# Two of the four weight sums of a seven-product block made by adding transfers instead of VectorE

## The chip, the cores and the metric

The kernel runs on one core of one Trainium2 chip. The metric is the device time of one execution in microseconds (us), given as the median of several runs. The profile is one further execution of the same program, with every instruction recorded.

## What is computed

Two layers of a hybrid language model on 256 tokens of width 1024, in fp32. Each layer is a feed-forward, a mixer (in the first layer a gated delta rule beside a state-space scan, in the second a sparse attention), and another feed-forward, each followed by a layer norm. So four of the six stages are this:

```python
def swiglu(x, w_in, w_out):
    gate, up = jnp.split(x @ w_in, 2, axis=-1)
    return (jax.nn.silu(gate) * up) @ w_out
# x: 256 x 1024, w_in: 1024 x 5632, w_out: 2816 x 1024
```

Weights come from HBM once per execution, 34.6 MB for one feed-forward.

## The kernel before

**Precision.** TensorE multiplies in a reduced fp32 form, so each operand is split into a high half (`whi`, a rounded copy, made on ScalarE or VectorE) and a low half (`wlo = raw - whi`, always VectorE), and each product is made of three matmuls: high by high, high by low, low by high. Every weight of 128 x 1024 thus costs one copy and one subtraction (`split`, line 657).

**A feed-forward** (`ffn`, line 986). The 2816 hidden columns are taken in units of 256. Most units ("R") load their gate and up columns, split them and multiply them with all tokens. Two places of each stage ("S" in `PATTERN`, line 49) take 512 columns at once with `block` (line 916): a scheme of Strassen's kind that makes the 2 x 2 blocks of (tokens) x (columns gate, up) with seven products instead of eight. `PATTERN` has one string for the first stage (one unit ahead of the pattern) and one for the other three. Eight blocks run in all.

**A block.** With b11, b12 the gate and up columns of the first 512 rows of the weights, and b21, b22 those of the second 512, the products take these weights, in this order: b11, T1, b21, T3, b22, T2, T4. The sums are made in place, one on the other, on tiles of raw weights:

```python
T1:  left  += right    # b11 + b12
T3:  right += b22      # b12 + b22
T2:  left  += b22      # T1 + b22
T4:  left  += b21      # T2 + b21
```

Each is done twice, for the two halves of k (`h` = 0, 1). A tile `r1` holds left (b11, columns 0 to 1023) and right (b12); `r2` holds b21 and b22. So a block holds four `raw` tiles of 1 MB, and there are just four buffers of that name (`RAW = 4`, line 27): further weights can only be loaded when T4 has been split. Left goes through the chain: b11 split, T1 added, T1 split, T2 added, T2 split, T4 added, T4 split. Right: T1 must have read it, then T3 is added and split. In before all four sums are `tensor_tensor` on VectorE (lines 935 to 942), of 128 x 1024 fp32. A product is twelve matmuls of 512 columns, six for each half of k. In the trace they read `whi,x` and `wlo,x` (b11, b21, T4) or `whi,sgh`, `wlo,sgh` and `whi,sgl` (T1, T3, b22, T2, with the token sums' halves `sgh` and `sgl`).

**What sets the order.** The kernel is first recorded as a list of operations (`Plan.add`), then `Plan.order` (line 328) plays it through with prices for each operation (`price`), waiting times between engines and a fixed number of buffers, and writes out one order for each engine; `emit` (line 559, the line of all instructions in the profile) issues them so. Within an engine everything runs strictly in that order, and an instruction that waits holds up all behind it. Copies recorded for ScalarE may be given to VectorE (`alts`) if VectorE is free first. A table (`ORDER`) corrects priorities by number of operation. Split weights live in tiles `m4`, at most 24 of them (12 pairs) for weights (`QUOTAS`, "W").

**Queues.** All loads are issued by SyncE. GpSimd has little to do: masks, a few powers for the layer norms (`lnve`), some attention work.

Of the kernel before, what the change touches and what calls it, by code (L numbers as in the profile page):

```python
# [9 lines left out]
F32 = mybir.dt.float32  # L10
# [3 lines left out]
OP = mybir.AluOpType  # L14
# [4 lines left out]
P = 128  # L19
T = 256  # L20
D = 1024
# [11 lines left out]
    "ps": (2, "PSUM"), "mp": (2, "PSUM"), "acc": (4, "PSUM"),  # L33
}

QUOTAS = {"M": None, "S": (8, 8), "Z": (4, 4), "L": (4, 4), "G": (4, 4), "P": (5, 5), "Q": (5, 5), "D": (4, 4), "W": (12, 24)}

KEPT = ("L", "G")

# [6 lines left out]

KEEP_WARM = 5500

PATTERN = {1: "RRRSRSRR", 2: "RSRRSRR"}


def H3(t, h):
# [120 lines left out]
class Plan:  # L173
# [76 lines left out]
    def price(self, op, eng, fn, args, kw):  # L250
        def n(a):
            return a.ids.size
        ps = lambda a: isinstance(a, V) and a.t.space == "PSUM"
        if eng == "tensor":
            out, l, r = args[:3]
            if fn == "transpose":
                return 111.0
            N, M = r.ids.size, l.ids.size
            if l.dtype == F32R:
                return N * 0.4427  # L260
            if M <= 32:
                return max(107.0, N * 0.455)
            if M <= 64:
                return 63.0 if N <= 64 else max(146.0, N * 0.896)
            return N * 1.7708 if N > M else 235.0 if N == M else 224.0
        if fn == "dma_start":
            return 60.0
        N = n(args[0]) if isinstance(args[0], V) else n(args[1])
        if isinstance(args[1] if len(args) > 1 else None, V):
            N = max(N, n(args[1]))  # L270
        ptr = sum(isinstance(kw.get(k), V) for k in ("scale", "bias"))
        if eng == "scalar":
            rows = args[0].p1 - args[0].p0

            more = (340 if rows <= 32 else 125 if rows <= 64 else 0) if fn == "activation" and N > 128 else 0
            return N / 1.2 + (51 if ps(args[1]) else 93) + 93 * ptr + (93 if "accum_out" in kw else 0) + more
        if eng == "vector":
            src = [a for a in args[1:] if isinstance(a, V)]
            if fn in ("tensor_copy", "tensor_scalar") and not any(ps(a) for a in src) and not ps(args[0]):
                c = N / (1.92 if N > 256 else 0.96) + 68  # L280
            elif fn == "reciprocal":
                c = N * 4 / 0.96 + 68
            elif fn == "memset":
                c = N / 0.96 + 20
            else:
                c = N / 0.96 + 67
            if fn == "tensor_tensor" and args[1].ids.ndim == 3 and N == 240:
                c += 165
            if fn == "scalar_tensor_tensor":
                c += 62 * isinstance(args[2], V)  # L290
            elif fn == "tensor_scalar":
                c += 62 * sum(isinstance(a, V) for a in args[2:4])
            return c
        if args[-1] is OP.pow:
            return 1300.0 + 130.0 * N
        return max(250.0, {"tensor_tensor": N * 2.1 + 150, "memset": N * .83 + 36,
                           "affine_select": N * .9 + 180}.get(fn, N * 1.7 + 480))
# [30 lines left out]
    def order(self, caps):  # L328
        ops = self.ops
        for op in ops:  # L330
            if op.fn == "dma_start":
                a = op.args[0] if isinstance(op.args[0], V) else op.args[1]
                op.nbytes = (a.p1 - a.p0) * a.ids.size * 4
                if isinstance(op.args[1], V) and op.args[1].t.space == "DRAM":
                    op.nbytes *= 2
            op.ndep = len(op.deps)
            op.ready = 0.0
# [18 lines left out]
        ready = {e: [] for e in engs}  # L356
        free = {e: 0.0 for e in engs}
        table = None
        dma_free = 0.0
        partial = heavy = False  # L360
        run = 0
        last = None
# [5 lines left out]
        left = len(ops)  # L368
# [62 lines left out]
        while left:  # L431
            best = None
            for e in engs:
# [7 lines left out]
                for op in lst:  # L441
                    r = op.ready
# [5 lines left out]
                    st = (r if r > f else f)  # L448
# [62 lines left out]
                port = st + c  # L511
            op.start = st
            if fn == "dma_start":
                dma_free = max(dma_free, st + 1300) + op.nbytes / 360.0
                op.end = dma_free + 600
                free[e] = st + c
            else:
                op.end = st + c
                free[e] = st + c
# [63 lines left out]
class K:  # L583
    NT = 2
    LAG = 5

    def __init__(self, plan, ins, caps):
        self.nc = self.plan = plan
# [327 lines left out]
    def block(self, st, w, c0, c1):  # L916

        nc, V = self.nc, self.nc.vector
        raw = []
        for h in range(2):  # L920
            tiles = [self.plan.tile("raw", [P, 2048], F32, "raw", stream="W") for r in range(2)]
            for r, t in enumerate(tiles):
                for e, c in enumerate((c0, c1)):
                    k = 4 * r + 2 * h
                    nc.sync.dma_start(t[:, e * 1024:(e + 1) * 1024].rearrange("p (k n) -> p k n", k=2),
                                      w[:, k:k + 2, c:c + 512])
            raw.append(tiles)
        A, B, C, D = (self.bank(tag) for tag in ("ps", "ps", "mp", "mp"))
        e1, e2 = self.m4(1024, "e1"), self.m4(1024, "e2")
        lh, rh = slice(0, 512), slice(512, 1024)  # L930

        def form(n, h):
            (r1, r2), u, v = raw[h], slice(0, 1024), slice(1024, 2048)
            left = r1[:, u]
            if n == "T1":
                V.tensor_tensor(left, left, r1[:, v], OP.add)
            elif n == "T3":
                V.tensor_tensor(r1[:, v], r1[:, v], r2[:, v], OP.add)
            elif n == "T2":
                V.tensor_tensor(left, left, r2[:, v], OP.add)  # L940
            elif n == "T4":
                V.tensor_tensor(left, left, r2[:, u], OP.add)
            src = {"b21": r2[:, u], "b22": r2[:, v], "T3": r1[:, v]}.get(n, left)
            hi, lo = self.m4(1024, "whi", "W", F32R), self.m4(1024, "wlo", "W", F32R)
            self.split(hi, lo, src)
            return hi, lo
# [39 lines left out]
    def ffn(self, l, j, x, then):  # L986
# [62 lines left out]
        def flush(keep):  # L1049
            while len(todo) > keep:  # L1050
                f, g, wo = todo.pop(0)
                out_mm(0, f, g, wo)
                if f >= NF - self.LAG:
                    late.append((f, g, wo))
                else:
                    out_mm(1, f, g, wo)
        st = None
        s = NT
        for n, kind in enumerate(PATTERN[NT]):
            if n == 3:  # L1060
                self.mark = len(self.plan.ops) - 1
            if kind == "S":
                if st is None:
                    st = self.sums_of_tokens(x)
                go = self.block(st, w_in, s * 256, DFF + s * 256)
                next(go)
                wo = self.unit_rows(w_out, 2 * s, 2, 0, D) + self.unit_rows(w_out, 2 * s + 2, 2, 0, D)
                flush(0)
                todo += [(2 * s + f, g, wo[f]) for f, g in enumerate(next(go))]
# [1 line left out]
                continue  # L1071
            wg = self.unit_cols(w_in, s * 256, 256)
            wu = self.unit_cols(w_in, DFF + s * 256, 256)
            if s == NT:
                for m in range(NT):
                    wo = self.unit_rows(w_out, 2 * m, 2, 0, D)
                    todo += [(2 * m + e, gts[2 * m + e], wo[e]) for e in range(2)]
            banks = self.proj_two(x, (wg[0], wu[0], wg[1], wu[1]), ("ps", "ps", "mp", "mp"))
            wo = self.unit_rows(w_out, 2 * s, 2, 0, D)
            for e in range(2):  # L1080
# [1192 lines left out]
```

## Time and profile before

| | |
|---|---|
| runs before | 1091.55, 1091.64, 1092.85 us; median 1091.64 |
| profiled execution | 1091.2 us |
| its span, first to last instruction | 1089.5 us |
| granted TensorE clock | 0.999 |
| instructions | 16005 |

How to read the profile: engines are PE (matmuls), PEld (weight loads, beside PE), DVE (VectorE), ACT (ScalarE), POOL (GpSimd), SP (SyncE; its q stands for its queue). `wlo<-raw,whi 128x1024 x390` names what an instruction writes and reads, the shape and the count; a group's row has busy us, mean ns of one, then the engine's idle time before them and who ended it. A timeline's row has start and length in us; a wait's row has us in total, times, longest. A DMA issue's row ends with the median time from issue to landing.

### The profile page before, as it was taken

What the parts mean: (1) busy time and instruction counts of PE and PEld (TensorE: products, weight loads), DVE (VectorE), ACT (ScalarE), POOL (GpSimd) and SP (SyncE); (2) the same over time, 40 slices, a digit from 0 to 9 for tenths busy, and PEclk for the clock granted to TensorE, in tenths of its full rate; (3) what the DMA queues carried; (4) which work ended last, traced back from release to release, by engine and by line L of the source; (5) the groups of instructions that cost most, each with busy time, mean ns of one, the idle gap of its engine ahead of it and who ended that gap; (6) DMA issues with size and microseconds to landing.
All of it is one profiled execution on the core that took longest, in us unless ns stands there. A gap on an engine that the chain in (4) does not pass through costs nothing.

```text
span 1089.5 us, 16005 instructions
## 1 busy us (share of the span) xinstructions
PE 1076.1 (99%) x6132; PEld 907.0 (83%) x6132; DVE 968.5 (89%) x1471; ACT 634.7 (58%) x1066; POOL 49.1 (5%) x78
## 2 busy tenths in 40 slices
PE   8999999999999999999999999999999999999997
PEld 6888888788999788888888888888887678888886
DVE  7999996888979899999995999897888999999965
ACT  5665673489788544555573655564375765655540
POOL 0000300001000110000000000010001000000000
PEclk9999999999999999999999999999999999999999
DMA  9919395633652383458394609378464145285541
GB/s 331 325 31 335 116 341 171 215 116 104 213 191 100 116 302 114 164 178 285 109 340 169 222 11 332 132 239 276 155 197 152 59 136 192 79 282 182 208 140 39
DMA packets 135799, 201.52 MB, mean 185 GB/s; under 512 B 10077, under 2 KB 95530, under 8 KB 135722
## 3 DMA queue, kind: packets, MB, share of 16 engines
q1 hardware_dynamic: 135722, 200.50, 54.2%
q8 instruction: 48, 0.79, 0.3%
q14 instruction: 29, 0.24, 0.1%
HBM read 197.18 MB, written 1.07 MB: 182 GB/s over the span
## 4 chain that ended last, share of the span: by engine, by line
PE 93%; DVE 3%; DMA 2%; ACT 1%; issue 1%; SPq 0%; DVEq 0%; ACTq 0%
PE ps L559 38%; PE acc L559 33%; PE mp L559 22%; DMA raw<-in_ffn_w_in_dram 1%; DVE arena L559 1%; DVE wlo L559 1%; DVE qs L559 0%; SPq L559 0%; DMA arena<-in_ssd_a_log_dram 0%; ACT whi L559 0%; DVE h L559 0%; DVE P L559 0%; DVE F L559 0%; ACT L559 0%; DVE g L559 0%
## 5 line engine op out<-in xcount | busy, mean ns | idle before, releaser
L559 DVE TENSOR_TENSOR wlo<-raw,whi 128x1024 fp32r<-128x1024 f32 (+1 forms) x396 | 469.0, 1213 | 10.2 <-ACT whi L559 7.7
L559 ACT ACTIVATE whi<-raw 128x1024 fp32r<-128x1024 f32 (+1 forms) x356 | 361.1, 1050 | 136.6 <-DMA raw<-in_ffn_w_in_dram 55.2
L559 PE MATMUL acc<-whi,g 128*128 128x512 f32 x704 | 223.3, 390 | 0.0
L559 PE MATMUL ps<-whi,x 128*128 128x512 f32 (+1 forms) x608 | 169.9, 386 | 1.3 <-DVE whi L559 1.3
L559 PE MATMUL ps<-x,whi 128*128 128x512 f32 (+1 forms) x720 | 159.2, 343 | 1.0 <-ACT cv L559 0.9
L559 PEld LDWEIGHTS acc<-whi,g 128*128 128x128 f32 x704 | 132.3, 188 | 26.7
L559 PE MATMUL acc<-wlo,g 128*128 128x512 f32 x352 | 137.4, 390 | 0.0
L559 PEld LDWEIGHTS ps<-x,whi 128*128 128x128 f32 x720 | 123.0, 189 | 17.2 <-ACT cv L559 2.4
L559 PEld LDWEIGHTS ps<-whi,x 128*128 128x128 f32 x608 | 109.7, 188 | 23.7 <-DVE whi L559 2.1
L559 PE MATMUL ps<-x,wlo 128*128 128x256 f32 x544 | 98.9, 284 | 0.0
L559 PE MATMUL ps<-wlo,x 128*128 128x512 f32 (+1 forms) x304 | 95.0, 385 | 0.5 <-DVE wlo L559 0.5
L559 PEld LDWEIGHTS ps<-x,wlo 128*128 128x128 f32 x544 | 81.1, 191 | 2.2 <-issue 0.2
L559 PE MATMUL mp<-x,whi 128*128 128x512 f32 x336 | 80.8, 390 | 0.2 <-DVE g L559 0.2
L559 ACT ACTIVATE sg<-ps 128x256 f32<-128x256 f32 x56 | 21.3, 380 | 95.6 <-PE ps L559 95.5
L559 PEld LDWEIGHTS acc<-wlo,g 128*128 128x128 f32 x352 | 66.2, 188 | 12.8
L559 PEld LDWEIGHTS mp<-x,whi 128*128 128x128 f32 x336 | 62.9, 188 | 13.6 <-DVE g L559 0.6
L559 DVE TENSOR_TENSOR sg<-ps,sg 128x256 f32<-128x256 f32 x56 | 23.4, 419 | 48.0 <-ACT sg L559 47.6
L559 PE MATMUL acc<-whi,x 128*128 128x512 f32 x192 | 65.3, 406 | 0.1
L559 PEld LDWEIGHTS ps<-wlo,x 128*128 128x128 f32 x304 | 55.5, 188 | 11.1 <-DVE wlo L559 1.0
L559 DVE TENSOR_TENSOR raw<-raw,raw 128x1024 f32<-128x1024 f32 x48 | 57.9, 1228 | 0.2
L559 PE MATMUL mp<-x,wlo 128*128 128x256 f32 x336 | 44.2, 283 | 0.0
L559 PEld LDWEIGHTS mp<-x,wlo 128*128 128x128 f32 x336 | 42.2, 192 | 0.2
(293 smaller groups left out, 1535.2 us busy)
## 6 DMA issues: line engine op xcount, KB each, us to landing
raw<-in_ffn_w_out_dram SPq DMA_DIRECT2D x44, 1024.0 KB, 5.0
raw<-in_ffn_w_in_dram SPq DMA_DIRECT2D x88, 512.0 KB, 5.3
raw<-in_ffn_w_in_dram SPq DMA_DIRECT2D x42, 1024.0 KB, 8.0
raw<-in_hyb_w_in_dram SPq DMA_DIRECT2D x20, 1024.0 KB, 6.0
raw<-in_hyb_w_out_dram SPq DMA_DIRECT2D x8, 1024.0 KB, 5.9
raw<-in_nsa_w_in_dram SPq DMA_DIRECT2D x5, 1024.0 KB, 5.9
raw<-in_nsa_w_out_dram SPq DMA_DIRECT2D x4, 1024.0 KB, 5.1
w<-in_nsa_cmp_w_dram SPq DMA_DIRECT2D x8, 512.0 KB, 9.0
```

The lines of the kernel that those rows point to most:

```text
L559: r = getattr(getattr(nc, eng), fn)(*[res(a) for a in args], **{k: res(a) for k, a in kw.items()})
```

## The change

T1 and T3 are no longer added by VectorE. GpSimd issues a transfer from one part of the raw tiles to another that adds to its destination (`accum_op=OP.add`), one for T1 and one for T3 in each half of k: 32 of 512 KB in the program. T2 and T4 stay on VectorE, and so do the splits of all. The tiles keep their layout (`HOME` says `raw` for both), `PATTERN` becomes a list by stage with the same strings, and the same steps are recorded in the same order. The planner's prices get a place for such a transfer.

```diff
-            return 60.0
+            return 1000.0 if eng == "gpsimd" else 60.0
...
-                dma_free = max(dma_free, st + 1300) + op.nbytes / 360.0
-                op.end = dma_free + 600
+                if e == "gpsimd":
+                    add_free = max(add_free, st + 1300) + op.nbytes / 360.0
+                    dma_free += op.nbytes / 360.0
+                    op.end = add_free + 600
+                else:
+                    dma_free = max(dma_free, st + 1300) + op.nbytes / 360.0
+                    op.end = dma_free + 600
...
+    HOME = ("raw", "raw")
+    RSTREAM = "R"
+    BY_DMA = ("T1", "T3")
...
-            (r1, r2), u, v = raw[h], slice(0, 1024), slice(1024, 2048)
-            left = r1[:, u]
-            if n == "T1":
-                V.tensor_tensor(left, left, r1[:, v], OP.add)
-            elif n == "T3":
-                V.tensor_tensor(r1[:, v], r1[:, v], r2[:, v], OP.add)
-            elif n == "T2":
-                V.tensor_tensor(left, left, r2[:, v], OP.add)
-            elif n == "T4":
-                V.tensor_tensor(left, left, r2[:, u], OP.add)
-            src = {"b21": r2[:, u], "b22": r2[:, v], "T3": r1[:, v]}.get(n, left)
+            left, right = part["b11", h], part["b12", h]
+            to, more = {"T1": (left, right), "T3": (right, part["b22", h]), "T2": (left, part["b22", h]),
+                        "T4": (left, part["b21", h])}.get(n, (None, None))
+            if to is not None:
+                if n in self.BY_DMA:
+                    nc.gpsimd.dma_start(to, more, accum_op=OP.add)
+                else:
+                    V.tensor_tensor(to, to, more, OP.add)
+            src = part.get((n, h), right if n == "T3" else left)
```

Since the planner's prices change, all engines' orders are made anew. TensorE's differs only in few rows at the ends of blocks, SyncE's in two loads. VectorE's has the 32 adds fewer, and 6 more copies of `whi`, one of `sgh`, 4 of `e` and 7 of `g` that ScalarE made before. Three places follow; numbers behind names tell tiles apart.

GpSimd, around the two blocks of the second feed-forward, before (`lnve` are the layer norms' powers, `arena_3706` the mixer's small values):

```order
L559 TENSOR_TENSOR arena_3706<-arena_3706,mhalf_110 128x1 x3
L559 TENSOR_TENSOR lnve_4250<-lnve_4250,mhalf_110 128x1
L559 TENSOR_TENSOR lnve_4364<-lnve_4364,mhalf_110 128x1
L559 TENSOR_TENSOR lnve_5841<-lnve_5841,mhalf_110 128x1
L559 TENSOR_TENSOR lnve_5939<-lnve_5939,mhalf_110 128x1
```

And after the change, the same place (`raw_4476` and `raw_4548` are left and right of the first block's two halves of k, `raw_4522` and `raw_4593` its b21 and b22; T1 has one tile on both sides):

```order
L564 TENSOR_TENSOR lnve_4364<-lnve_4364,mhalf_110 128x1
L564 DMA raw_4476<-raw_4476 128x1024
L564 DMA raw_4476<-raw_4522 128x1024
L564 DMA raw_4548<-raw_4548 128x1024
L564 DMA raw_4548<-raw_4593 128x1024
L564 DMA raw_5012<-raw_5012 128x1024
L564 DMA raw_5075<-raw_5075 128x1024
L564 DMA raw_5012<-raw_5037 128x1024
L564 DMA raw_5075<-raw_5117 128x1024
L564 TENSOR_TENSOR lnve_5841<-lnve_5841,mhalf_110 128x1
```

Eight transfers stand between two layer norms. In the first block T3 of the first half (which must wait for T1's landing there, as it overwrites what T1 reads) comes ahead of T1 of the second half; in the second block both T1 come first.

VectorE, first block of the second feed-forward, from the low half of b11 to that of T1, before (`whi_4644` is T1's high half, `xf` and `sgl` belong to the token sums):

```order
L559 TENSOR_TENSOR wlo_4562<-raw_4476,whi_4534 128x1024
L559 TENSOR_TENSOR g_4486<-mp_4558,g_4486 128x128 x2
L559 TENSOR_TENSOR xf_4440<-xf_4455,xf_4440 128x512
L559 TENSOR_TENSOR wlo_4580<-raw_4183,whi_4316 128x1024
L559 TENSOR_TENSOR xf_4455<-xf_4455,xf_4440 128x512
L559 TENSOR_TENSOR sgl_4598<-xf_4440,sgh_4582 128x1024
L559 TENSOR_TENSOR xf_4455<-xf_4455 128x512
L559 TENSOR_TENSOR wlo_4611<-raw_4548,whi_4589 128x1024
L559 TENSOR_TENSOR raw_4476<-raw_4476 128x1024
L559 TENSOR_TENSOR sg_4628<-ps_4540,sg_4628 128x256
L559 TENSOR_TENSOR sgl_4642<-xf_4455,sgh_4614 128x1024
L559 TENSOR_TENSOR sg_4628<-ps_4569,sg_4628 128x256
```

And after (`whi_4626` is T1's high half):

```order
L564 TENSOR_TENSOR wlo_4562<-raw_4476,whi_4534 128x1024
L564 TENSOR_TENSOR g_4486<-mp_4558,g_4486 128x128 x2
L564 TENSOR_TENSOR xf_4440<-xf_4455,xf_4440 128x512
L564 TENSOR_TENSOR wlo_4581<-raw_4183,whi_4316 128x1024
L564 TENSOR_TENSOR xf_4455<-xf_4455,xf_4440 128x512
L564 TENSOR_TENSOR sgl_4599<-xf_4440,sgh_4583 128x1024
L564 TENSOR_TENSOR xf_4455<-xf_4455 128x512
L564 TENSOR_TENSOR wlo_4612<-raw_4548,whi_4590 128x1024
L564 TENSOR_TENSOR sgl_4629<-xf_4455,sgh_4615 128x1024
L564 TENSOR_TENSOR wlo_4644<-raw_4476,whi_4626 128x1024
L564 TENSOR_TENSOR sg_4639<-ps_4540,sg_4639 128x256
L564 TENSOR_TENSOR sg_4639<-ps_4569,sg_4639 128x256
```

The add of T1 is gone, its low half has moved ahead of the `sg` sums that empty the banks of the unit before, and eight rows now stand between b11's low half and T1's. On ScalarE the copy `whi_4626` likewise stands ahead of the four copies that empty those banks. Further on in this block the cast of T1's other half stands eleven rows behind `wlo_4644`, and T3's other low half six rows behind that cast.

VectorE, second block of the same stage, before (left of the two halves is `raw_5027` and `raw_5108`):

```order
L559 TENSOR_TENSOR wlo_5126<-raw_5027,whi_5090 128x1024
L559 CAST whi_5136<-raw_5108 128x1024
L559 TENSOR_TENSOR raw_5027<-raw_5027 128x1024
L559 TENSOR_TENSOR wlo_5147<-raw_5108,whi_5136 128x1024
L559 TENSOR_TENSOR raw_5027<-raw_5027,raw_5063 128x1024
L559 TENSOR_TENSOR wlo_5164<-raw_5027,whi_5151 128x1024
L559 TENSOR_TENSOR raw_5108<-raw_5108 128x1024
```

And after (left is `raw_5012` and `raw_5075`):

```order
L564 TENSOR_TENSOR wlo_5115<-raw_5012,whi_5094 128x1024
L564 TENSOR_TENSOR wlo_5129<-raw_5075,whi_5121 128x1024
L564 CAST whi_5155<-raw_5012 128x1024
L564 TENSOR_TENSOR wlo_5162<-raw_5012,whi_5155 128x1024
L564 TENSOR_TENSOR raw_5012<-raw_5012,raw_5037 128x1024
L564 TENSOR_TENSOR wlo_5184<-raw_5075,whi_5176 128x1024
```

Between b11's low half and the cast of T1, which reads what the transfer has added, one row is left.

More of the change, by code (lines that the diff above doesn't have):

```diff
@@ L34 @@
 }
[L36 removed]
+QUOTAS = {"M": None, "S": (8, 8), "Z": (4, 4), "L": (4, 4), "G": (4, 4), "P": (5, 5), "Q": (5, 5), "D": (4, 4), "W": (12, 24), "R": (8, 8)}
 KEPT = ("L", "G")
@@ L47 @@
 KEEP_WARM = 5500
-PATTERN = {1: "RRRSRSRR", 2: "RSRRSRR"}
+PATTERN = ["RRRSRSRR", "RSRRSRR", "RSRRSRR", "RSRRSRR"]
 def H3(t, h):
@@ L333, in order @@
                 op.nbytes = (a.p1 - a.p0) * a.ids.size * 4
-                if isinstance(op.args[1], V) and op.args[1].t.space == "DRAM":
+                if isinstance(op.args[1], V) and (op.args[1].t.space == "DRAM" or op.eng == "gpsimd"):
                     op.nbytes *= 2
@@ L358, in order @@
         table = None
-        dma_free = 0.0
+        dma_free = add_free = 0.0
         partial = heavy = False
@@ L918, in block @@
         nc, V = self.nc, self.nc.vector
-        raw = []
+        part = {}
         for h in range(2):
-            tiles = [self.plan.tile("raw", [P, 2048], F32, "raw", stream="W") for r in range(2)]
-            for r, t in enumerate(tiles):
+            for r in range(2):
+                pair = None
+                if self.HOME[r] == "raw":
+                    pair = self.plan.tile("raw", [P, 2048], F32, "raw", stream="W")
                 for e, c in enumerate((c0, c1)):
                     k = 4 * r + 2 * h
-                    nc.sync.dma_start(t[:, e * 1024:(e + 1) * 1024].rearrange("p (k n) -> p k n", k=2),
-                                      w[:, k:k + 2, c:c + 512])
-            raw.append(tiles)
+                    t = pair[:, e * 1024:(e + 1) * 1024] if pair is not None else self.m4(1024, "raw", self.RSTREAM)
+                    nc.sync.dma_start(t.rearrange("p (k n) -> p k n", k=2), w[:, k:k + 2, c:c + 512])
+                    part["b%d%d" % (r + 1, e + 1), h] = t
         A, B, C, D = (self.bank(tag) for tag in ("ps", "ps", "mp", "mp"))
@@ L1056, in flush, with first @@
                     out_mm(1, f, g, wo)
+        def first():
+            for m in range(NT):
+                wo = self.unit_rows(w_out, 2 * m, 2, 0, D)
+                todo.extend((2 * m + e, gts[2 * m + e], wo[e]) for e in range(2))
         st = None
         s = NT
-        for n, kind in enumerate(PATTERN[NT]):
+        self.count = getattr(self, "count", -1) + 1
+        for n, kind in enumerate(PATTERN[self.count]):
             if n == 3:
@@ L1066, in ffn @@
                 next(go)
+                if n == 0:
+                    first()
                 wo = self.unit_rows(w_out, 2 * s, 2, 0, D) + self.unit_rows(w_out, 2 * s + 2, 2, 0, D)
@@ L1073, in ffn @@
             wu = self.unit_cols(w_in, DFF + s * 256, 256)
[L1074 to L1077, printed above, removed]
+            if n == 0:
+                first()
             banks = self.proj_two(x, (wg[0], wu[0], wg[1], wu[1]), ("ps", "ps", "mp", "mp"))
```

## Prediction

> **What bounds the kernel now.** I read the page first, for the engines' shares of the span.
>
> ```profile
> span 1089.5 us, 16005 instructions
> PE 1076.1 (99%) x6132; PEld 907.0 (83%) x6132; DVE 968.5 (89%) x1471; ACT 634.7 (58%) x1066; POOL 49.1 (5%) x78
> PE 93%; DVE 3%; DMA 2%; ACT 1%; issue 1%; SPq 0%; DVEq 0%; ACTq 0%
> ```
>
> TensorE is busy for 99% of the span. Since ends of matmuls are modelled, that alone proves little, so the next view is what TensorE waits for, whole.
>
> ```profile
> PE ps L559 <- DVE whi L559: 1.3, 1, 1.3
> PE acc L559 <- POOL ones L559: 1.1, 1, 1.1
> PE ps L559 <- ACT cv L559: 0.9, 1, 0.9
> PE ps L559 <- DVE wlo L559: 0.5, 1, 0.5
> PE mp L559 <- DVE P L559: 0.4, 1, 0.4
> PE mp L559 <- DVE e L559: 0.3, 1, 0.3
> PE ps L559 <- ACT P L559: 0.3, 1, 0.3
> PE mp L559 <- DVE arena L559: 0.3, 1, 0.3
> PE mp L559 <- DVE g L559: 0.2, 1, 0.2
> ```
>
> All waits add up to 5.3 us. Those on VectorE are 1.3 + 0.5 (both once, for the first weights of the program), 0.4 + 0.3 (attention), and 0.3 + 0.2 at the `e` and `g` tiles, which blocks and their neighbours make. Only the last 0.5 us lies where the change works. The chain of waits shows the pace inside a block; this row is one run of 36 matmuls of 512 columns, the products with a11, T1 and a12:
>
> ```profile
> 529.61 8.16 PE ps L559 x36
> ```
>
> 8.16 / 36 = 0.227 us from one matmul to the next, without a hole. So in feed-forward stages the end is set by TensorE's own matmuls, and the change adds or removes none.
>
> How near VectorE is to being late is read from one block, the first one of the second feed-forward. The table by stages of 10 us gives busy times in the order PE, PEld, DVE, ACT, POOL, then the granted clock, the DMA share and GB/s:
>
> ```profile
> 450.00:460.00 10.00, 10.00 (x60) 8.90 (x59) 9.76 (x16) 5.83 (x11) 0.00 (x0) 1.00 0.25 92
> 460.00:470.00 10.00, 10.00 (x46) 8.28 (x45) 10.00 (x10) 4.74 (x7) 0.00 (x0) 1.00 0.00 0
> ```
>
> VectorE works 9.76 and 10.00 of 10 us; the DMA engines fall to a share of 0.25 and then to nothing, since all four `raw` buffers are held by the block. What VectorE's pace costs is seen by pairing the end of a low half (`wlo`) with the matmul that reads it, in the timelines of VectorE and TensorE:
>
> ```profile
> 454.90 1.23 DVE L559 TENSOR_TENSOR wlo<-raw,whi 128x1024 fp32r<-128x1024 f32 x1
> 468.39 0.39 PE L559 MATMUL ps<-wlo,sgh 128*128 128x512 f32 x1
> 480.24 1.23 DVE L559 TENSOR_TENSOR wlo<-raw,whi 128x1024 fp32r<-128x1024 f32 x1
> 483.35 0.39 PE L559 MATMUL mp<-wlo,x 128*128 128x512 f32 x1
> 539.93 1.22 DVE L559 TENSOR_TENSOR wlo<-raw,whi 128x1024 fp32r<-128x1024 f32 x1
> 547.36 0.39 PE L559 MATMUL mp<-wlo,x 128*128 128x512 f32 x1
> 131.20 2.36 DVE L559 TENSOR_TENSOR wlo<-raw,whi 128x1024 fp32r<-128x1024 f32 x2 [1.22 <-ACT whi L559]
> 136.06 0.39 PE L559 MATMUL mp<-wlo,x 128*128 128x512 f32 x1
> ```
>
> The low half of T1 (first half of k) is done at 456.13 and read at 468.39: a lead of 12.3 us. The block's last low half, of T4, is done at 481.47 and read at 483.35: a lead of 1.9 us. So VectorE loses 10 us against TensorE over this block, and yet nobody waits. The last low half of the second block of that stage has 547.36 - 541.15 = 6.2 us, that of the second block of the first feed-forward 136.06 - 133.56 = 2.5. VectorE is the second bound, close behind, but behind.
>
> **The change part by part.** *Adds removed.* The groups of instructions hold them:
>
> ```profile
> L559 DVE TENSOR_TENSOR raw<-raw,raw 128x1024 f32<-128x1024 f32 x48 | 57.9, 1228 | 0.2
> L559 DVE TENSOR_TENSOR raw<-raw 128x1024 f32<-128x1024 f32 x16 | 19.3, 1218 | 0.1
> L559 DVE CAST whi<-raw 128x1024 fp32r<-128x1024 f32 x39 | 26.6, 687 | 1.8 <-DMA raw<-in_ffn_w_in_dram 0.8 <-DMA raw<-in_ffn_w_out_dram 0.5
> L559 ACT ACTIVATE whi<-raw 128x1024 fp32r<-128x1024 f32 x351 | 357.1, 1053 | 136.1 <-DMA raw<-in_ffn_w_in_dram 55.2 <-DVE raw L559 35.1 <-DMA raw<-in_ffn_w_out_dram 33.9
> L559 DVE COPY PT<-mp 128x512 f32<-128x512 f32 x10 | 6.8, 686 | 2.2 <-PE mp L559 2.0
> L559 DVE CAST g<-sg 128x256 fp32r<-128x256 f32 x9 | 2.6, 291 | 0.2
> ```
>
> The 16 adds with one name on the right are T1 (both operands in one tile). The 48 are T2, T3 and T4, of which T3 is 16. So 16 x 1.218 + 16 x 1.228 = 39.1 us leave VectorE, 4.9 us a block. (Adds in a row start 1.13 us apart, so 4 x 1.13 = 4.5 us of a block's time.)
>
> *Copies moved.* With VectorE freer, the planner gives it more of the copies that ScalarE did: 6 of `whi` and one of `sgh` at 0.687 us (the cast's row), 4 of `e` and 3 of `g` with 512 columns at 0.686 (nearest row, the copy PT<-mp), 4 small ones of `g` at 0.291. That is 4.8 + 4.8 + 1.2 = 10.8 us back on VectorE. Net 39.1 - 10.8 = 28.3 us less: 968.5 becomes about 940.
>
> *Worth of that.* TensorE waits for VectorE 0.5 us in these stages, so the most that 28.3 us can buy is 0.5 us. The rest only lengthens leads. I take 0.3.
>
> *The transfers added.* 32 transfers of 512 KB from SBUF to SBUF that read the destination as well. No row of before is one, nor any transfer from GpSimd's queue. The nearest rows, with the time from issue to landing at the end:
>
> ```profile
> Y<-zeros SPq DMA_DIRECT2D x2, 512.0 KB, 3.8
> raw<-in_ffn_w_in_dram SPq DMA_DIRECT2D x88, 512.0 KB, 5.3
> raw<-in_ffn_w_in_dram SPq DMA_DIRECT2D x42, 1024.0 KB, 8.0
> w<-in_nsa_cmp_w_dram SPq DMA_DIRECT2D x8, 512.0 KB, 9.0
> ```
>
> Y<-zeros is a plain SBUF to SBUF transfer of that size: 3.8 us, the lower end (it can't be cheaper with a second read). Twice the bytes is like the 1024 KB rows, 8.0 us, and a crowded 512 KB takes 9.0, the upper end. During a block the DMA engines are mostly idle (0.25 and 0.00 above), so I start from the first row and add what 512 KB more cost from HBM: 3.8 + (8.0 - 5.3) = 6.5 us. L = 6.5 is an estimate, and GpSimd's issue is in it only so far as SP's is.
>
> [...]
>
> *What covers L.* In the first block of the second feed-forward the new order puts eight rows of VectorE between the low half of b11 and that of T1. They are in the trace of before, with their starts:
>
> ```profile
> 445.95 0.48 DVE L559 TENSOR_TENSOR g<-mp,g 128x128 fp32r<-128x128 f32 x2
> 451.56 1.21 DVE L559 TENSOR_TENSOR raw<-raw 128x1024 f32<-128x1024 f32 x1
> 453.33 1.22 DVE L559 TENSOR_TENSOR sgl<-xf,sgh 128x1024 fp32r<-128x1024 f32 x1
> 454.46 0.42 DVE L559 TENSOR_TENSOR sg<-ps,sg 128x256 f32<-128x256 f32 x1
> ```
>
> From 445.95 (the two `g`) to 451.56 is 5.61, and the last of them, `sgl`, takes 454.46 - 453.33 = 1.13: 6.7 us. ScalarE's high half of T1 (1.05 us) must fit in too, and hand-overs, so about 5.4 us of L are covered. The second place is T3 of the other half of k, with five rows between it and T1's cast there, so about 5.0 covered. The third is T1 of the other half, which GpSimd issues only after T3 of the first, so after the first landing: some 7 us. With L = 6.5 VectorE waits 1.1 + 1.5 + 0 = 2.6 us in such a block. Against that stand the 4.5 us of adds that are gone and a lead of 1.9, 6.4 us in all. The lead grows by some 2 us.
>
> In the second blocks only the low half of b11's other half (1.13 us) stands between. There VectorE stands still for L - 1.1 = 5.4 us, 0.9 more than the adds took (4.5), and the lead of 6.2 shrinks to 5.3.
>
> *Who is queued behind these waits.* On ScalarE, behind the high half of T1, stand the copies that empty four banks of the projection before. In before VectorE empties one of them at 452.99, and TensorE writes a `ps` bank again at 465.44:
>
> ```profile
> 452.99 0.42 DVE L559 TENSOR_TENSOR sg<-ps,sg 128x256 f32<-128x256 f32 x1 [0.22 <-ACT sg L559]
> 465.44 0.39 PE L559 MATMUL ps<-whi,x 128*128 128x512 f32 x1
> ```
>
> 12 us of room hide a wait of one. On GpSimd, behind a transfer that waits, stand only the block's other transfers; the powers of the layer norms come after a block's last one. On SP nothing moves but two weight loads by a few places. The next loads wait for the `raw` buffers, and these come free when T4's low half is done, as before or earlier.
>
> *Sum.* The profiled execution took 1091.2 us, 1.7 over its span, and the median of the three runs is 1091.64. 1091.64 - 0.3 + 0 = 1091.3 us. A measurement of this kernel tells about 0.2% (2.2 us) from no change, so this is no change.
>
> **The rivals.** *Slow landing: slower.* If L is larger, VectorE, in order, stands still with all other low halves behind the wait, and beyond the lead TensorE stops. In the first block of the second feed-forward it waits (L - 5.4) + (L - 5.0) + (L - 7.0), which reaches 6.4 at L = 7.9: from there on the time grows. At L = 9.0 (the crowded row) that block loses 3.2 us and the second block of the first feed-forward, whose lead is nearly as small (2.5), about 3: 1091.3 + 6 = 1097. At L = 10 these two lose 6 each and two further blocks 3 each: 1109. For it: no row shows an adding transfer, and the three waits add up. Against it: the DMA engines are mostly idle then, and the rows that read most like it stay under 7.9 save in a crowd. Chance 0.26.
>
> [...]
>
> *TensorE isn't the bound: faster.* The chain gives VectorE 3% of the span, of which the low halves of weights are:
>
> ```profile
> by line: PE ps L559 38.4%; PE acc L559 32.9%; PE mp L559 22.0%; DMA raw<-in_ffn_w_in_dram 1.3%; DVE arena L559 0.6%; DVE wlo L559 0.6%; issue 0.5%; DVE qs L559 0.5%; SPq L559 0.4%; DMA arena<-in_ssd_a_log_dram 0.3%; ACT whi L559 0.3%; DVE h
> ```
>
> 0.6% or 6.5 us. If these are real, relief of VectorE returns up to 6.5 us: 1085. [...] Against it stand the 0.227 us without a hole and the waits of 5.3 us; the chain steps aside into VectorE where TensorE goes on. Chance 0.07.
>
> *The order shifts something elsewhere.* A few TensorE rows swap places at each block's end, which is worth tenths. It stays in the forecast's case.
>
> **The numbers.** Forecast (no change) 0.67, slow landing 0.26, faster 0.07. Of the slow case about half lies above L = 9.3 (1099), 0.12 left out; below 1089.5 about 0.07. So the range is 1089.5 to 1099, and most of it is the slow case's; the forecast's own range is 1089.5 to 1093. Faster 0.07, same 0.67, slower 0.26.
>
> **What would show it.** In the profile of the changed kernel: `raw<-raw` with 16 gone from VectorE and 32 of `raw<-raw,raw` left, 45 casts of `whi`, VectorE near 940 us; 32 issues of 512 KB on POOL, landing after some 6.5 us; gaps of VectorE of some 5 us that end on those landings in the second block of the last three feed-forwards, and of 1 to 2 us in first blocks; TensorE's waits still near 5 us with `e` and `g` perhaps gone. I am wrong if TensorE waits for `whi` or `wlo` inside blocks (slow landing: look at the landing time, 8 us or more), or if the span drops by over 2.2 us (then TensorE's rows hid stalls).

## The result, and the profile after

| | before | after |
|---|---|---|
| median | 1092.24 us (4 runs, 1091.55 to 1094.99) | 1102.2 us (4 runs, 1099.69 to 1103.28) |
| profiled execution | 1091.2 us, span 1089.5 | 1102.02 us, span 1100.3 |
| granted TensorE clock | 0.999 | 0.996 |

The ratio is 1.0083 with a 95% interval of 1.0058 to 1.0108. The kernel is slower by 9 us, 0.8%, four times what a measurement can tell from no change. (Ratios and medians leave disturbed runs out, in all one of g2's; a ratio is not taken from the medians and can differ a little from theirs.)

The page of the changed kernel, for shares of the span, then its groups and its issue row for what was moved:

```profile
PE 1080.5 (98%) x6132; PEld 909.1 (83%) x6132; DVE 945.0 (86%) x1457; ACT 622.3 (57%) x1048; POOL 73.5 (7%) x110
```

```profile
L564 DVE TENSOR_TENSOR raw<-raw,raw 128x1024 f32<-128x1024 f32 x32 | 39.4, 1235 | 0.5
L564 DVE CAST whi<-raw 128x1024 fp32r<-128x1024 f32 x45 | 30.9, 689 | 28.3 <-DMA raw<-raw 19.2 <-DMA raw<-in_ffn_w_out_dram 6.9 <-DMA raw<-in_ffn_w_in_dram 1.8
```

```profile
raw<-raw POOLq DMA_DIRECT2D x32, 512.0 KB, 5.5
```

The edit did what it says: 32 adds are left, six more casts of `whi`, VectorE is busy for 945.0 us instead of 968.5, and 32 transfers land after 5.5 us in the median. But TensorE's waits, whole, are 11.6 us where they were 5.3, and the new ones have one name:

```profile
PE mp L564 <- DVE e L564: 4.6, 3, 2.6
PE ps L564 <- DVE e L564: 1.8, 1, 1.8
```

Where they lie is told by the table by stages (busy time of PE, PEld, DVE, ACT, POOL, then the granted clock, the DMA share and GB/s). Nearly all of the loss is in one place, the second block of the first feed-forward and the units behind it. Before:

```profile
120.00:130.00 10.00, 10.00 (x46) 8.29 (x45) 9.45 (x11) 6.26 (x8) 9.64 (x7) 1.00 0.41 85
130.00:140.00 10.00, 10.00 (x46) 8.29 (x45) 8.76 (x10) 3.30 (x4) 0.64 (x4) 1.00 1.02 354
140.00:150.00 10.00, 9.49 (x46) 7.27 (x44) 9.29 (x13) 8.75 (x11) 0.00 (x0) 1.00 0.94 317
150.00:160.00 10.00, 10.00 (x59) 8.94 (x60) 10.00 (x14) 7.79 (x14) 0.00 (x0) 1.00 0.97 350
```

After:

```profile
120.00:130.00 10.00, 8.21 (x33) 6.34 (x32) 9.97 (x10) 5.33 (x6) 6.79 (x10) 0.89 0.11 21
130.00:140.00 10.00, 10.00 (x43) 8.18 (x42) 9.02 (x11) 5.29 (x6) 0.00 (x0) 0.94 0.54 133
140.00:150.00 10.00, 8.47 (x40) 6.80 (x39) 6.11 (x9) 3.16 (x4) 0.00 (x0) 1.00 1.05 368
150.00:160.00 10.00, 7.39 (x28) 5.67 (x27) 9.96 (x12) 9.24 (x10) 0.00 (x0) 0.83 1.01 342
```

The slices count 144 matmuls in these 40 us instead of 197 (one that spans two slices counts in both). Two things besides its waits are to be seen. The granted clock is 0.89, 0.94 and 0.83 in slices that hold or follow a wait: it is 0.50, half of what it was, from 127.84 to 131.25 us and from 155.15 to 158.56. And the DMA engines, at a share of 1.02 from 130 to 140 before, are at 0.54: loads that should run there do not.

One number for each kernel helps below. I take the starts of TensorE's matmuls, and sum by how much each stands further from the next than is usual for its shape (the lower quartile, from 40 ns over it on); from 120 to 205 us this **stall** is 1.6 us before and 10.2 after. Over the whole program it is 58.0 and 68.8, so this place holds 8.6 of 10.8 us, and the span grew by 10.8. (Most of the rest, 1.3 us, is lost ahead of 40 us. The three waits shown below add up to 5.9 us; two times 3.41 us at half the clock lose another 3.4.)

What happens there, in order. GpSimd's issues (start, length, what it waited for), then ScalarE's first copy behind them:

```profile
104.75 0.86 POOL L564 DMA_DIRECT2D raw<-raw  x1 [41.71 <-DMA raw<-in_ffn_w_in_dram]
108.25 0.86 POOL L564 DMA_DIRECT2D raw<-raw  x1 [2.64 <-DVE sg L564]
114.25 0.86 POOL L564 DMA_DIRECT2D raw<-raw  x1 [5.14 <-DMA raw<-raw]
116.71 0.86 POOL L564 DMA_DIRECT2D raw<-raw  x1 [1.60 <-DMA raw<-raw]
```

```profile
113.98 1.06 ACT L564 ACTIVATE whi<-raw 128x1024 fp32r<-128x1024 f32 x1 [4.01 <-DMA raw<-raw]
```

T1's transfer of 104.75 lands only at 113.96, after 9.21 us (three loads of this block, which land at 107.64, 110.17 and 112.79, are under way too, and from 108.25 on T1's other transfer); that of T3 at 114.25 has no load beside it and lands after 4.65. ScalarE and VectorE stand still for about 4 us, so the sums on VectorE come later. T4's two adds, before:

```profile
125.61 2.35 DVE L559 TENSOR_TENSOR raw<-raw,raw 128x1024 f32<-128x1024 f32 x2
```

And after:

```profile
129.06 1.23 DVE L564 TENSOR_TENSOR raw<-raw,raw 128x1024 f32<-128x1024 f32 x1
132.67 1.22 DVE L564 TENSOR_TENSOR raw<-raw,raw 128x1024 f32<-128x1024 f32 x1
```

Before, the second starts at 126.75, right behind the first. The first is 3.5 us late, of which the kernel brought 1.3 along from its start; the second is 5.9 late, since the new order also puts two low halves between them. Then SyncE, before:

```profile
119.70 0.59 SPq L559 DMA_DIRECT2D arena<-in_gdn_conv_w_dram  x1
...
125.22 1.01 SPq L559 DMA_DIRECT2D arena<-in_hyb_w_in_dram  x2
126.90 1.50 SPq L559 DMA_DIRECT2D raw<-in_ffn_w_out_dram  x2
```

And after:

```profile
130.35 0.37 SPq L564 DMA_DIRECT2D raw<-in_ffn_w_out_dram  x1
130.84 0.59 SPq L564 DMA_DIRECT2D arena<-in_gdn_conv_w_dram  x1
...
136.55 1.06 SPq L564 DMA_DIRECT2D arena<-in_hyb_w_in_dram  x2
137.71 1.01 SPq L564 DMA_DIRECT2D raw<-in_ffn_w_out_dram  x1
138.83 1.03 SPq L564 DMA_DIRECT2D raw<-in_ffn_w_in_dram  x2
```

Before, eleven small loads for the next stage (`arena`) went out one after the other from 119.70 to 126.2, SyncE issued nothing else in between, and both w_out loads followed at 126.90 and 128.03, when T4's adds had freed their buffers. After, the first w_out load stands ahead of the eleven. It waits on SyncE until its buffer is free at 130.35, the eleven come behind it, and the second w_out load goes out at 137.71, 9.7 us later than before, though VectorE has read its buffer for the last time at 132.75. The three loads behind it follow in one heap. VectorE and TensorE, at the end of that block:

```profile
143.89 0.69 DVE L564 CAST whi<-raw 128x1024 fp32r<-128x1024 f32 x1 [4.67 <-DMA raw<-in_ffn_w_out_dram]
144.50 0.68 DVE L564 TENSOR_TENSOR e<-mp,e 128x512 f32<-128x512 f32 x1
147.37 0.68 DVE L564 TENSOR_TENSOR e<-ps,e 128x512 f32<-128x512 f32 x1
```

```profile
126.81 0.50 PE L564 MATMUL ps<-whi,x 128*128 128x512 f32 x1 [1.79 <-DVE e L564]
149.31 0.66 PE L564 MATMUL mp<-ident,e 128*128 128x128 f32 x4 [1.53 <-DVE e L564]
154.65 0.68 PE L564 MATMUL mp<-ident,e 128*128 128x128 f32 x4 [2.61 <-DVE e L564]
```

VectorE, in order, stands 4.67 us in front of a cast that needs the late load, the sums of `e` are behind it, and TensorE waits for these: 1.53 and 2.61 us. The wait of 1.79 us at 126.81 is another: the copy that empties the bank of a11 and a12 was ScalarE's before and now stands on VectorE behind two low halves.

### The profile page after: what moved, and what is told of

It is laid out like the page before. It is cut to its first block, busy times and chain, and to the rows that moved or that the text cites. A ratio compares the mean times of both kernels' runs of the same rounds, so it can differ in the third digit from the quotient of the medians.

```text
span 1100.3 us, 16129 instructions
## 1 busy us (share of the span) xinstructions
PE 1080.5 (98%) x6132; PEld 909.1 (83%) x6132; DVE 945.0 (86%) x1457; ACT 622.3 (57%) x1048; POOL 73.5 (7%) x110
## 3 DMA queue, kind: packets, MB, share of 16 engines
q0 software_dynamic: 4608, 16.78, 8.1%
## 4 chain that ended last, share of the span: by engine, by line
PE 88%; DVE 5%; DMA 3%; issue 1%; ACT 1%; SPq 0%; DVEq 0%; ACTq 0%
PE ps L564 37%; PE acc L564 31%; PE mp L564 21%; DVE wlo L564 2%; DMA raw<-in_ffn_w_in_dram 2%; DMA raw<-raw 1%; DMA raw<-in_ffn_w_out_dram 1%; DVE arena L564 1%; ACT whi L564 0%; DVE qs L564 0%; DVE e L564 0%; SPq L564 0%; DVE raw L564 0%; DVE h L564 0%; DVE whi L564 0%
## 5 line engine op out<-in xcount | busy, mean ns | idle before, releaser
L564 ACT ACTIVATE whi<-raw 128x1024 fp32r<-128x1024 f32 (+1 forms) x350 | 353.6, 1049 | 166.1 <-DMA raw<-raw 54.0
L564 DVE CAST whi<-raw 128x1024 fp32r<-128x1024 f32 (+1 forms) x46 | 31.5, 687 | 28.3 <-DMA raw<-raw 19.2
L564 POOL DMA_DIRECT2D raw<-raw x32 | 28.1, 891 | 360.7 <-DMA raw<-in_ffn_w_in_dram 210.4
```

Source lines behind the costliest of these rows:

```text
L564: r = getattr(getattr(nc, eng), fn)(*[res(a) for a in args], **{k: res(a) for k, a in kw.items()})
```

## The experiments

All ran beside the kernel before on the same chip; ratios are to it, with 95% intervals (in the four groups e, f, g and h it took 1092.55, 1094.01, 1092.14 and 1091.86 us). "SyncE's row" says whether the first w_out load stands ahead of the eleven small loads or behind them.

| run | transfers | SyncE's row | stall 120-205 | span over before | DMA share 130-140 | median us | ratio |
|---|---|---|---|---|---|---|---|
| before | 0 | behind | 1.6 | | 1.02 | 1092.24 | |
| after | 32 | ahead | 10.2 | 10.8 | 0.54 | 1102.2 | 1.0083 (1.0058 to 1.0108) |
| e1_not_first | 24 | behind | 1.0 | -0.2 | 1.02 | 1092.74 | 0.9997 (0.9982 to 1.0013) |
| e2_first_only | 8 | ahead | 7.1 | 10.2 | 0.71 | 1101.53 | 1.0078 (1.0054 to 1.0101) |
| e3_order_alone | 0 | ahead | 9.6 | 18.8 | 0.39 | 1111.16 | 1.0181 (1.0147 to 1.0214) |
| e4_transfers_alone | 64 | behind | 6.9 | 53.8 | 0.96 | 1147.89 | 1.0502 (1.0472 to 1.0533) |
| f4_transfers_32 | 32 | behind | 3.0 | 16.0 | 0.91 | 1109.38 | 1.0139 (1.0103 to 1.0175) |
| f1_copy_first | 32 | ahead | 7.1 | 5.8 | 0.76 | 1101.37 | 1.0070 (1.0048 to 1.0092) |
| f2_casts_behind | 32 | ahead | 7.4 | 10.1 | 0.63 | 1099.97 | 1.0050 (1.0034 to 1.0067) |
| f3_both | 32 | ahead | 9.4 | 10.0 | 0.57 | 1099.95 | 1.0051 (1.0031 to 1.0071) |
| g1_load_behind | 32 | behind | 3.0 | 2.9 | 1.02 | 1094.37 | 1.0035 (1.0016 to 1.0053) |
| g2_load_and_rows | 32 | behind | 3.2 | 4.4 | 0.94 | 1096.38 | 1.0042 (1.0019 to 1.0065) |
| g3_price_3000 | 32 | behind | 4.8 | 5.0 | 0.35 | 1099.29 | 1.0065 (1.0040 to 1.0091) |
| h1_before_load_ahead | 0 | ahead | 5.9 | 8.0 | 0.75 | 1098.74 | 1.0055 (1.0034 to 1.0077) |

The profiled span is set against before's 1089.5 us. f1's profile is of its fastest execution (1097.04 us) and g3's of one of its faster ones (1096.25), so their rows are low for their medians. The stall of this place is not all that the spans lose. Matched one by one with before, the 6132 starts of TensorE's matmuls in e2, f2 and h1 fall back by 2.9, 3.5 and 3.1 us more between 300 and 320 us, in the first layer's mixer: TensorE stands still there once, for 1.3 to 1.8 us, where the profile names no engine that it waits for, and the granted clock is 0.83 from 310 to 320 us (before 1.00). The changed kernel has none of it, and whether it belongs to these changes no run settles.

**Where.** Two kernels split the change by stage.

```diff
-                if n in self.BY_DMA:
+                if n in self.BY_DMA and self.count > 0:     # e1; in e2: == 0
```

> The two blocks of the first feed-forward keep all adds on VectorE; the six blocks of the other three make T1 and T3 by transfer. Theory A (the loss is local: in the first feed-forward's second block the transfers share the DMA engines with the block's own loads, land after 8 to 9 us, and the delay is handed on through the raw buffers to the next loads): 1092 us within 1.5, and VectorE's waits on landings in the other feed-forwards still there without harm. Rival C (each transfer costs its share, 10 us over 32): 24 of 32 left, so about 1099.7. Rival B (the order that the planner makes for VectorE with fewer adds) says nothing here, since that order goes too.

> The other way round: only the two blocks of the first feed-forward make T1 and T3 by transfer (8 transfers), the other six blocks add on VectorE. Theory A: about 1101, the whole loss, with the clock below 1 between 120 and 160 us as in the changed kernel. Rival C (each transfer its share): 8 of 32, about 1094.7.

1092.74 and 1101.53: the loss needs only the first feed-forward's transfers, and 24 in the other three cost nothing. (Of the 10.2 us of e2's span, 5.7 are lost in the place and 2.9 in the mixer.) This is not because they land sooner. In e1 the first transfer of the second feed-forward's second block goes out at 508.64 and takes 8.08 us, those of the other two such blocks 7.4, and VectorE waits for the landings:

```profile
DVE whi L564 <- DMA raw<-raw: 19.4, 5, 5.9
```

In e2, T1's transfers in the bad block took 7.7 and 7.8 us, and it lost as much. So the same landing costs nothing in one place and much in another; a late landing alone doesn't explain it.

**Order or transfers.** In e3 the changed kernel's order is kept, and VectorE adds again at the transfers' places.

```diff
+                if fn == "dma_start" and eng == "gpsimd":
+                    eng, fn, args, kw = "vector", "tensor_tensor", (args[0], args[0], args[1], OP.add), {}
                 r = getattr(getattr(nc, eng), fn)(...)
```

> The changed kernel's order on every engine, planned with transfers, but each adding transfer is replaced by VectorE's add at the same place of the program. No transfer is left. Theory A: the loss begins with the late landings, so without them 1092 to 1094 (VectorE has the 39 us of adds again and 10.8 us of copies besides, which the leads may not cover everywhere). Rival B (the new order of VectorE, with copies of e moved there and a cast put ahead of the sums of e, is what holds TensorE): 1099 or more, with waits of TensorE for e between 120 and 160 us.

1111.16. The place is as bad as in the changed kernel, with a stall of 9.6 us and no transfer in the program. It holds 8.1 of the 18.8 us by which the span grew; 2.6 are lost ahead of it in the same feed-forward, and 7.4 in the other three. Theory A began the loss with the landings; it falls, since the place is lost without any, and rival B, the order, has the number. But VectorE has the adds and the moved copies at once here (busy for 979.6 us), so e3 does not part the order from a late VectorE, and it doesn't say which rows. TensorE's waits:

```profile
PE mp L566 <- DVE e L566: 8.8, 5, 4.1
PE ps L566 <- DVE e L566: 2.8, 2, 1.7
```

The opposite, the order of before with transfers in the place of adds, was tried twice. In e4 my edit caught T2 and T4 too, since they share an operand with T1, so 64 sums were transfers:

```diff
+                if fn == "tensor_tensor" and id(args[0]) in BY_QUEUE:      # f4: id(args)
+                    eng, fn, args, kw = "gpsimd", "dma_start", (args[0], args[2]), {"accum_op": OP.add}
                 r = getattr(getattr(nc, eng), fn)(...)
```

> The order of the kernel before on every engine, planned with VectorE's adds, but the 32 adds of T1 and T3 are taken out of VectorE's row and issued as adding transfers by GpSimd at the same place of the program. No copy is moved to VectorE. Theory A: the landings of 8 to 9 us in the first feed-forward's second block are late here too and the raw buffers come free as late: 1096 to 1101, lost between 100 and 160 us. Rival B (the order): about 1092. Since in this order fewer rows of VectorE stand between an add and its reader than in the changed kernel, other blocks may lose some us as well by the rows of leads (1.9 us at T4 of the second feed-forward's first block); that would be told by the place.

> What e4 was meant to be: the order of the kernel before on every engine, with the 32 adds of T1 and T3 alone issued as transfers at the same places. In that order only a row or two of VectorE stand between such an add and its reader. Theory A2 (the landing has to be covered by the order, and the planner's new order covers it outside the first feed-forward): slower than the changed kernel, 1105 to 1130, and lost in all four feed-forwards. Rival B (the new order is the harm, the transfers are not): 1092.

With 64 transfers 1147.89, which says nothing of T1 and T3 alone. With 32 1109.38, as theory A2 had it in size, but not in place: the third feed-forward loses nothing and the first little (a stall of 3.0, 1.4 over before), the stage of the second has a stall of 6.8 us (470 to 640 us; before 1.0), and waits for `g` (3.3 us once) and `e` stand in the last. So the planner's new order is what covers the landings there, and in the first feed-forward that order holds something bad which the order of before does not.

**VectorE's and ScalarE's rows.** Three kernels move single rows of the order in the bad block: f1 VectorE's copy ahead of two low halves, f2 a cast and two low halves on VectorE and two copies on ScalarE behind the sums and the Silu of `e`, f3 both.

```diff
+            held = [order[n] for n in (857, 864)]                              # f1
+            order = order[:857] + order[858:864] + order[865:872] + held + order[872:]
```

> The changed kernel with one row moved: in the first feed-forward's second block VectorE's copy of the bank of a11 and a12 (at 126.07 us in the changed kernel) stands ahead of two low halves that it stood behind. TensorE's wait of 1.96 us for it at 124.62 should go, and the slow clock behind it (0.89 from 120 to 130 us). Theory A2 (TensorE's end is set there by the late raw buffers, through the load that VectorE and ScalarE wait for at 143.9): the time gained is lost again in longer waits for e at 147 to 155 us, 1101 to 1102. Rival B2 (each wait of TensorE counts by itself): 1102.2 - 2 for the wait - 2 for the clock = 1098.

> The changed kernel with the other rows moved: in the same block VectorE's cast and two low halves of the w_out unit that lands at 143.9 us, and ScalarE's two copies of the w_in unit that lands at 146.9, stand behind the sums of e and behind ScalarE's Silu of e, which they stood ahead of. The waits for e of 1.5 and 2.6 us at 149 and 154.7 should go, with the slow clock behind them (0.83 from 150 to 160 us). Theory A2: this is the place that counts; 1102.2 - 4.1 - 2.5 = about 1095.5, and the 1.8 us wait for the copy at 126 stays. Rival C (the transfers cost by their number, the order nothing): 1102.

> Both moves together, all 32 transfers as in the changed kernel. Theory A2: the waits for e between 120 and 160 us are gone and the time is 1092 to 1093, within 0.2% of the kernel before, though the transfers land as late as ever (T1 of that block 8 to 9 us). Rival C: 1102. A time between 1095 and 1099 would say that the late weights themselves, not the rows in front of e, hold TensorE.

1101.37, 1099.97 and 1099.95. f1 went as A2 said: the wait at 126 is gone, and the longest of those for `e` behind it is 3.6 us instead of 2.6. f2 wins some 2 us by the medians and 3.6 by the ratios (1.0050 for 1.0083), of the 6.7 that A2 gave. f3 shows that these rows aren't the main cause. The waits for `e` shrink to 1.7 us, and in their place stands one for the late weights themselves:

```profile
PE ps L575 <- ACT whi L575: 3.6, 1, 3.6
PE mp L575 <- DVE e L575: 1.7, 3, 1.3
```

Its result lies outside what A2 gave (1092 to 1093). (T1 landed after 9.74 and 9.29 us in this execution, later than in the changed kernel's.) A2 falls as well: which row waits is, as I read it, only the form that the late loads take. That left SyncE.

**SyncE's row.** In g1 one row moves: the w_out load is put behind the eleven small loads.

```diff
+            order = order[:899] + order[900:925] + [order[899]] + order[925:]
```

> The changed kernel with one row of SyncE moved: in the first feed-forward the w_out load that waits at 130.35 us for its raw buffer stands behind the eleven small loads of the next stage again, as in the kernel before, instead of ahead of them. In the changed kernel these eleven then take SyncE until 137.0, and the second w_out load goes out at 137.71, though its buffer is free at 132.75. Theory A3 (this is the step that hands the late transfers on to the next loads): the second w_out load goes out at about 132.8 and lands near 140 instead of 143.9, the w_in load behind it near 142 instead of 146.9; the waits for e of 1.5 and 2.6 us and the slow clock behind them go, the 1.8 us wait for the copy at 126 stays: 1102.2 - 4.1 - 2.5 = about 1095.5. Rival B2 (the rows of VectorE and ScalarE in front of e do it): 1101 to 1102.

1094.37 with all 32 transfers. SyncE now, and the stages that were bad:

```profile
125.61 2.19 SPq L566 DMA_DIRECT2D arena<-in_hyb_w_in_dram  x2
127.96 2.61 SPq L566 DMA_DIRECT2D raw<-in_ffn_w_out_dram  x2
```

```profile
130.00:140.00 10.00, 10.00 (x46) 8.28 (x45) 9.46 (x12) 4.70 (x6) 0.49 (x3) 1.00 1.02 361
140.00:150.00 10.00, 8.42 (x42) 6.73 (x41) 10.00 (x14) 9.08 (x10) 0.00 (x0) 1.00 1.07 360
150.00:160.00 10.00, 10.00 (x61) 8.90 (x60) 10.00 (x15) 7.07 (x13) 0.00 (x0) 1.00 0.94 322
```

The second w_out load goes out at 130.20 and lands at 136.91; the DMA share from 130 to 140 us is 1.02 again and the clock 1.00, though T1's transfers took 7.75 and 7.61 us. The stall falls from 10.2 to 3.0. T1 landed up to 1.5 us sooner here than in the changed kernel's profile; e2, with the row ahead and landings of 7.68 and 7.81, is the closer pair, and has a stall of 7.1. With the rows of f3 besides (g2) nothing more is won:

> SyncE's row moved as in g1, and VectorE's and ScalarE's rows as in f3, all 32 transfers as in the changed kernel. Theory A3: f3 took the rows away and left TensorE waiting 3.6 us for weights that come late; with the load early too, 1092 to 1093.5 and no wait over 1 us between 120 and 160 us. If the transfers themselves cost something that no order hides, 1097 or more.

1096.38, a miss by 3 us; TensorE still waits 2.0 us for `e` once. The reverse is the sharper test: the kernel before, with no transfer at all, and only SyncE's row as the changed kernel has it (the eleven behind the load, and the exponential that reads one of them behind two copies).

```diff
+            order = order[:902] + [order[n] for n in range(902, 933) if n not in small and n != 922] \
+                    + [order[n] for n in small] + order[933:968] + [order[922]] + order[968:]
```

> The kernel before, without any transfer, with SyncE's row put as the changed kernel has it: the w_out load that waits at 126.90 us for its raw buffer stands ahead of the eleven small loads (and the exponential on ScalarE that reads one of them stands behind the two copies that it stands behind in the changed kernel). The eleven then take SyncE from 127 to about 133, and the second w_out load goes out near 133 instead of 128.03 and lands near 139 instead of 135.4. Theory A3, part one (the row costs by itself, whatever made the buffers late): 2 to 4 us, 1094 to 1096, with TensorE waiting for e or whi between 135 and 150 us. Theory A3, part two (the row costs only when the transfers have made the buffers late already): 1092.

```profile
126.95 0.37 SPq L567 DMA_DIRECT2D raw<-in_ffn_w_out_dram  x1
127.41 0.58 SPq L567 DMA_DIRECT2D arena<-in_gdn_conv_w_dram  x1
...
133.01 1.06 SPq L567 DMA_DIRECT2D arena<-in_hyb_w_in_dram  x2
134.19 0.91 SPq L567 DMA_DIRECT2D raw<-in_ffn_w_out_dram  x1
```

```profile
PE mp L567 <- DVE e L567: 4.8, 3, 2.8
145.71 0.66 PE L567 MATMUL mp<-ident,e 128*128 128x128 f32 x4 [2.78 <-DVE e L567]
140.00:150.00 10.00, 5.66 (x26) 4.08 (x25) 8.33 (x10) 6.68 (x7) 0.00 (x0) 1.00 1.08 369
```

1098.74, ratio 1.0055: the first w_out load goes out when it always did, the second 6.2 us later (134.19 for 128.03), and TensorE waits 4.8 us for `e`, of which 2.78 and 1.70 in the same place as in the changed kernel. Some 6 us of loss without any transfer, more than I gave it. By the profile 4.4 us are lost in the place and 3.1 in the mixer; if the latter is not the row's doing, the row costs some 4 us, the upper end of what I gave.

**The planner told of a longer landing.**

```diff
-                    op.end = add_free + 600
+                    op.end = add_free + 3600
```

> Nothing moved by hand: the planner is told that an adding transfer takes 3.0 us longer (some 8.2 us instead of 5.2 until its reader may start, about what T1 takes in the first feed-forward's second block) and makes all orders anew. It puts the small loads first on SyncE again and the two w_out loads behind them. Theory A3 (the loss is the planner's order, made for a landing that is too short): 1091.5 to 1094. Rival: the landing itself, 1099 or more, whatever the order.

1099.29, a miss. The planner does put the load behind the eleven, but it also moves T4's adds back, to 134.09 and the row behind; the buffers come free later still, and both w_out loads go out at 135.38 and 136.51 (DMA share 0.35 from 130 to 140). Another road to the same end: late loads.

## Why the prediction was wrong

- *TensorE bounds the kernel.* Right. e1 takes 24 adds from VectorE and the time doesn't move (0.9997), so the rival "faster" falls as well. The busy time (99%) and the waits (5.3 us) told the bound rightly here.
- *Work removed and moved.* Nearly: VectorE fell to 945.0 us, not 940, with the 45 casts of `whi` that were named.
- *Copies moved, priced as busy time alone.* Too low: one of them, in front of a bank that TensorE needs, is the wait of 1.79 us. With it undone (f1) the time is not clearly better (1.0070 against 1.0083), since the late loads come behind it.
- *Landing, L = 6.5.* 5.5 in the median, from 4.5 to 9.2. The two transfers that run alone, at 470.90 and 651.02 us, take 4.53 and 4.55. The 2.7 us in L for a second read of 512 KB were my estimate, and no run shows them: the profile counts 16.78 MB for the 32 transfers, 512 KB each. What I had wrong is "during a block the DMA engines are mostly idle": that was read at 450 to 470 us in before, when the block's loads had landed (the last at 453.11). T1 of a second block is issued while one to four of its own block's loads are under way, and takes 6.5 to 9.2. Two that go out close together take long as well: those of 642.25 and 642.91 us in a first block, with no load under way, take 6.04 and 7.82. Beside loads alone the transfer of 456.74 takes 5.29 (one to three loads under way) and that of 637.40 4.56 (one load, until 638.97). How loads and transfers share the DMA engines no run shows.
- *Covers and leads.* Right in six blocks of eight: VectorE's gaps of up to 5.9 us in second blocks, foretold as some 5, cost nothing (e1). An L of 8.08 did no harm there either; the threshold of 7.9 was worked out for a first block, with three such landings in a row.
- *The failed step* is "Who is queued behind these waits": "On SP nothing moves but two weight loads by a few places. The next loads wait for the `raw` buffers, and these come free when T4's low half is done, as before or earlier." One of the moves took a w_out load past eleven others on an in-order queue, to the head, where it waits for a buffer until 130.35; the eleven go out behind it, from 130.84. (The other, of two layer-norm loads, is in e1 too and costs nothing.) I counted its places and not what it now stands in front of, nor what a second load behind the eleven would lose. And the buffers did not come free as before: T4's two adds ended at 130.3 and 133.9 instead of 126.8 and 128.0, since in this block L is not covered and the new order parts the two. In the sum this lies in the "+ 0", which came to some 9 us. The prediction had a rival for it, *The order shifts something elsewhere*, but looked at TensorE's rows alone and priced it at tenths. h1 shows the first alone costs 0.55% (0.34 to 0.77); g1 shows that without it 0.35% (0.16 to 0.53) of the 0.83% are left.
- *Rival slow landing.* It had the sign, and the place (the second block of the first feed-forward) among its two; its price, 6 us, came near by luck: by the prediction's own rule for second blocks (L - 1.1 against 4.5 of adds and a lead of 2.5) an L of 9.0 costs 0.9 us there, not "about 3". Its mechanism, low halves that reach TensorE too late from L = 7.9 on, is not what happened: TensorE's waits there are for `e`, and with SyncE's row put right (g1) an L of 7.6 and 7.8 costs a stall of 1.4 us over before; with the row wrong (e2), 7.7 and 7.8 cost 5.5.

What stays open: the 0.35% that g1 leaves. Its profile shows 1.6 us of wait for `e` in the block and 1.0 us in the second feed-forward; neither was undone by itself. Why the planner sends the load first was not tried either, beyond g3, where a longer landing in its model turns the row back.

No kernel here beats the kernel before. The best with transfers, e1, equals it.

## What to carry to other kernels

A change to one engine's work can also change the order of every in-order queue that waits for that work: look first at what a waiting instruction now stands in front of, SyncE's loads above all, and price the queue behind it, not the number of places moved. Here eleven small loads stood behind one that waited, and the second w_out load went out at 137.71 instead of 128.03. The other feed-forwards took landings nearly as late for nothing, and no w_out load had moved ahead of others there. That their loads have more room is not the reason: behind the second block of the second feed-forward they run as densely (a DMA share of 1.05 and 1.01 from 540 to 560 us before). What a late load would cost there no run shows. An idle resource read in one window says nothing of the window in which the new work will be issued: T1 of the second blocks went out beside one to four loads.

## What the runs showed of the hardware

An adding transfer of 512 KB within SBUF took GpSimd 0.86 us to issue in the median (0.85 to 1.15). It landed after 4.53 and 4.55 us where it ran alone, after 7.82 beside another adding transfer issued 0.66 us ahead of it, and after up to 9.21 beside three loads of 512 KB and another adding transfer.

The wait of 1.79 us before 126.81 cost TensorE more than it lasted: behind it the matmuls of 512 columns were slow for 3.4 us:

```profile
129.10 0.63 PE L564 MATMUL ps<-wlo,x 128*128 128x512 f32 x1
129.53 1.05 PE L564 MATMUL ps<-whi,x 128*128 128x512 f32 x2
130.38 0.63 PE L564 MATMUL ps<-wlo,x 128*128 128x512 f32 x1
```

129.10 to 129.53 is 0.43 us from one to the next instead of 0.227, and the granted clock is 0.50 from 127.84 to 131.25 us. At half the clock these 3.41 us lose another 1.7, an estimate from the two numbers. It is not so behind every such wait: behind the 1.53 us before 149.31 in the same profile, the 1.58 in g1 and the 2.78 and 1.70 in h1 the granted clock stays at 1.00 (in the changed kernel until 155.15, behind the next wait). What decides between the two is not shown.
